# Gate steps four deep, one per piece, and lo products first in every other piece of a two-block network

## The chip, the cores and the metric

One core of one Trainium2 chip. The metric is device microseconds of one launch; lower is better. All weights come from HBM in float32 during the launch.

## What is computed

Two transformer-like blocks run on 256 tokens of width 2048. The part that the change touches is the expert layer of the second block: 16384 experts, of which each token uses 8 heads x 16. The kernel computes it densely.

```python
def peer(xn, w_pq, sub_k1, sub_k2, expert_u, expert_v):
    q = (xn @ w_pq).reshape(B, S, PEER_HEADS, 2, PEER_HALF)
    s1 = einsum('bshd,hnd->bshn', q[..., 0, :], sub_k1)
    s2 = einsum('bshd,hnd->bshn', q[..., 1, :], sub_k2)
    v1, i1 = top_k(s1, 16); v2, i2 = top_k(s2, 16)
    cand = v1[..., :, None] + v2[..., None, :]
    vs, ci = top_k(cand.reshape(..., 256), 16)
    eidx = e1 * 128 + e2            # e1, e2: entries of i1, i2 that ci names
    gates = softmax(vs)
    act = gelu(einsum('tkd,td->tk', expert_u[eidx], xb))
    return einsum('tk,tkd->td', act * gates, expert_v[eidx])
```

Before it stand a first block (three mixers, a feed-forward part of width 5632 with `w_up` and `w_dn`) and the attention of the second block; behind it a gated projection. None of that is changed, except that `w_up` uses the same product routine as the expert layer.

## The kernel before

**Products.** Every weight matrix is read in pieces of 512 KB (128 x 1024 float32). SyncE loads a piece into `raw` (line 327), ScalarE rounds it to `hi` (line 341), VectorE takes `lo = raw - hi` (line 342), and TensorE multiplies with the activations, which are split the same way. `get` (line 345) splits two pieces ahead; `raw`, `hi` and `lo` have three buffers each. In `mmH` (line 382; used by `w_up`, `w_pq` and `w_u`: 176, 32 and 256 pieces) a piece is 8 long products of 512 columns (line 390: `hi` times both halves of the activations) and then 8 short products of 256 columns (line 393: `lo` times the high half). Four pieces make one product [128, 2, 512] in `mm`; `sum_halves` (line 403) adds its halves with one ScalarE copy and two VectorE operations.

**Work beside the products.** `Background` holds generators (tasks). After each piece `pump` (line 71) lets them go on, in the order of the list, while two budgets last: `bg.rate` units (a rough cost in us) per piece for VectorE and as many for ScalarE. A plain `yield` hands back the turn within the same pump, `yield 1` waits for the next pump, and `finish` (line 98) runs a task to its end without a product in between. What the pump calls is written into the instruction queues at that point; each engine runs its queue in order.

**The expert layer** (`peer`, line 1832). Around the 32 pieces of `w_pq` and in the first part of `w_u` the routing runs: scores, top 16 (VectorE max, index and replace), pairs. Then `dense` makes the gates as a dense array of 256 tokens x 16384 experts in DRAM (`gdram`), in 64 steps of four tokens. One step: VectorE compares an iota with the tokens' indices (`AB`, 128 x 1024) and scales a quarter of it (128 x 256), ScalarE scales another quarter (two of 128 x 128), TensorE multiplies the two one-hot halves (line 1983: four float32 products of 128 columns, which the trace records as eight), ScalarE evicts `m` into `G`. Each fourth step completes a `G` of 1 MB, which ScalarE's queue stores to `gdram`. In the kernel before, the one-hot of step n+1 is made behind the product of step n, and the eviction of n behind that, with a plain `yield` between.

`peer_order` (line 1144): 16 quads of `w_u` (8 pieces each: 128 pieces), then the two products `v` with `w_v` (16 pieces each), then two quads and one `v` in turn. `gated` (line 2006) turns each quad's activations into factors of `v`: gelu on ScalarE, then, once all gates are stored, a load `Gq` from `gdram` by SyncE's queue, a VectorE product, and a split into `wh` and `wl`. At the first `v`, `finish` runs what is left of `dense`, then `gated` of quads 0 and 1.

Of the kernel before, what the change touches and what calls it, by code (L numbers as in the profile page):

```python
# [6 lines left out]
F32 = mybir.dt.float32  # L7
# [4 lines left out]
AF = mybir.ActivationFunctionType  # L12
# [235 lines left out]
class Net:  # L248
# [132 lines left out]

    def mmH(self, ps, hi, lo, k0, X, first, last):

        nc = self.nc
        kk, n = hi.shape[1:]
        kw = dict(skip_group_check=True)
        sl = [slice(c0, c0 + 128) for c0 in range(0, n, 128)]
        for i in range(kk):
            for c in range(n // 128):
                nc.tensor.matmul(ps[:, c], hi[:, i, sl[c]], X.both(k0 + i), start=first and i == 0, stop=False, **kw)  # L390
        for i in range(kk):
            for c in range(n // 128):
                nc.tensor.matmul(ps[:, c, 256:], lo[:, i, sl[c]], X(k0 + i)[0], start=False, stop=last and i == kk - 1, **kw)  # L393

    def prodH(self, name, X, nk, kk=4):
        ps = self.mm_ps([128, 2, 512])
# [1434 lines left out]
class Block3(Block2):  # L1831
    def peer(self, X):
        nc, V, S, G, A, bg, tc = self.nc, self.V, self.S, self.G, self.A, self.bg, self.tc
        V.fixed = 0.15
        bg.rate = 2.8
        h, st = self.h, self.st
        pa_ = ExitStack()
        pact = pa_.enter_context(tc.tile_pool(name="act", bufs=NACT))
# [92 lines left out]
        r_ = self.a4([128, 3, 256], name="routeT")  # L1931
# [23 lines left out]
        gst = {"ready": False}  # L1955

        def dense():

            yield lambda: t_route[3]
            rp_.close()  # L1960
            gp_ = gst["ctx"] = ExitStack()
            gp = gst["pool"] = gp_.enter_context(tc.tile_pool(name="gates", bufs=1, reuse_waits="tile"))
            def onehot(n):

                AB = gp.tile([128, 2, 4, 128], F32, name="AB", tag="AB", bufs=2)
                V.tensor_tensor(AB, self.iota[:, None, None, :].to_broadcast([128, 2, 4, 128]),
                                r_[:, 0:2, 4 * n:4 * n + 4, None].to_broadcast([128, 2, 4, 128]), op=OP.is_equal)
                V.tensor_mul(AB[:, 0, 0:2], AB[:, 0, 0:2], r_[:, 2, 4 * n:4 * n + 2, None].to_broadcast([128, 2, 128]))
                for i in (2, 3):
                    S.activation(AB[:, 0, i], AB[:, 0, i], AF.Copy, scale=r_[:, 2, 4 * n + i:4 * n + i + 1])  # L1970
                return AB

            bg.rate = 3.3
            nxt, full = onehot(0), None
            for n in range(64):
                if n % 4 == 0:
                    g = gp.tile([128, 128, 16], F32, name="G", tag="G", bufs=2)
                yield
                yield self.hold("m1")
                ps = self.m1([128, 4, 128])  # L1980
                AB = nxt
                for i in range(4):
                    nc.tensor.matmul(ps[:, i], AB[:, 1, i], AB[:, 0, i], start=True, stop=True)  # L1983
                if full is not None and n % 4 == 2:
                    nc.scalar.dma_start(self.gdram[n // 4 - 1], full.rearrange("p e t -> p (e t)"))
                    full = None
                if n < 63:
                    yield
                    nxt = onehot(n + 1)
                yield  # L1990
                S.activation(g[:, :, 4 * (n % 4):4 * (n % 4) + 4], ps.rearrange("p t e -> p e t"), AF.Copy)
                self.drop("m1")
                if n % 4 == 3:
                    full = g
            yield 1
            nc.scalar.dma_start(self.gdram[15], full.rearrange("p e t -> p (e t)"))
            yield 4
            gst["ready"] = True
            bg.rate = RATE

        t_route = bg.add(route())
        bg.add(dense())
        W, wt = {}, {}
        self.room.update(W=2, Gq=3)

        def gated(qd, a):
            S.activation(a, a, AF.Gelu_apprx_tanh)
            yield lambda: gst["ready"]
            yield self.hold("W")
            yield self.hold("Gq")  # L2010
            gq = gst["pool"].tile([128, 16, 4, 16], F32, name="Gq", tag="Gq", bufs=3)
            nc.sync.dma_start(gq.rearrange("p b e t -> p b (e t)"),
                              self.gdram.rearrange("b p n -> p b n")[:, :, 64 * qd:64 * qd + 64])
            yield 2
            V.tensor_mul(a.rearrange("p e (b t) -> p e b t", b=16), a.rearrange("p e (b t) -> p e b t", b=16),
                         gq.rearrange("p b e t -> p e b t"))
            self.drop("Gq")
            yield 1
            hi = self.a4([128, 4, 256], R32, "wh")
            lo = self.a4([128, 4, 256], R32, "wl")  # L2020
            S.activation(hi, a, AF.Copy)
            yield 1
            V.tensor_sub(lo, a, hi.bitcast(F32))
            W[qd] = hi, lo
# [4 lines left out]
        for kind, i in self.peer_order():  # L2029
            if kind == "u":  # L2030
                for z in range(2):
                    ps = self.prodH("w_u", X, 16)
                    if z == 0:
                        if i >= FIRST:
                            bg.finish(wt[i - NACT])
                        a = self.a4([128, 4, 256], name="act") if i < FIRST - NACT else pact.tile([128, 4, 256], F32, name="act")
                    self.sum_halves(a[:, 2 * z:2 * z + 2], ps, st["R4"])
                wt[i] = bg.add(gated(i, a))
                bg.tasks.insert(sum(not w[3] for w in wt.values()) - 1, bg.tasks.pop())
                continue  # L2040
            for qd in (2 * i, 2 * i + 1):
                bg.finish(wt[qd])
            Wf = lambda k: (W[2 * i + k // 4][0][:, k % 4], W[2 * i + k // 4][1][:, k % 4])
            for c in range(4):
                ps = self.prodB("w_v", Wf, 8)
                V.tensor_add(h[c], h[c], ps)
                if i == 15:
                    X5.make(c, lambda t, c=c: h[c][:, t], lambda j, c=c: self.col("g_ple", 4 * c + j),
                            before=self.squares(h[c], ssp[:, :, c:c + 1]))
            self.room["W"] += 4 if i == 1 else 2  # L2050
            del W[2 * i], W[2 * i + 1]
# [81 lines left out]
```

## Time and profile before

| | before |
|---|---|
| median of 3 runs | 3577.65 us (3572.88 to 3577.75) |
| the profiled execution's own time | 3569.16 us |
| its span, first to last instruction | 3567.4 us |
| mean granted TensorE clock | 0.994 of full speed |
| PE, DVE, ACT busy | 98%, 68%, 48% of the span |

A busy share is the mean over stages that have different limits. The layer in question runs from about 1850 us of the span to its end; the gate steps stand between 2137 and 2383 us. In a row of the timeline, "x8" is a group of eight instructions that follow each other; the number before the engine is the time from the first one's start to the last one's end, which overlaps the next group's start, so rates are read from start to start.

### The profile page before, as it was taken

The page shows a single profiled execution, that of the slowest core. Times are in us where ns is not written, and L with a number is a line of the kernel's source. Part 1 is how long each engine was busy: PE and PEld are TensorE (multiplying, and loading weights), DVE is VectorE, ACT ScalarE, POOL GpSimd, SP SyncE. Part 2 cuts the span into 40 slices and gives each one's busy share as a digit, 9 for nine tenths or more (in the row PEclk, how much of TensorE's full clock was granted, in tenths as well). Part 3 has the DMA queues.
Part 4 walks back from the last instruction along what each step waited for, and adds up shares of the span by engine and source line. Part 5 has one row for each costly group of instructions (what it writes and reads, how often), then busy time and mean ns, then how long its engine had stood idle before and what let it go on. Part 6 is the DMA issues. An engine that isn't in the chain of part 4 may idle for free.

```text
span 3567.4 us, 47459 instructions
## 1 busy us (share of the span) xinstructions
PE 3494.6 (98%) x18330; PEld 2983.6 (84%) x18330; DVE 2431.3 (68%) x3152; ACT 1712.7 (48%) x2100; POOL 268.9 (8%) x358
## 2 busy tenths in 40 slices
PE   8999999999999999999999999979999999999999
PEld 8788877888888888889788888867888888888887
DVE  7997675566775577667669987765656666666665
ACT  4345543445554455545554445543444444444453
POOL 6900000000000000020212000000000000000000
PEclk9999999999999999999999999989999999999999
DMA  6454554655566555665455555556766666667755
GB/s 227 152 162 161 171 171 141 198 199 184 188 201 194 190 191 186 193 192 176 135 171 180 186 183 178 189 175 195 214 206 202 201 202 203 205 203 216 220 189 183
DMA packets 244795, 670.05 MB, mean 188 GB/s; under 512 B 86181, under 2 KB 86629, under 8 KB 242393
## 3 DMA queue, kind: packets, MB, share of 16 engines
q1 hardware_dynamic: 239144, 639.59, 56.6%
q10 hardware_dynamic: 2736, 17.32, 1.2%
q0 software_dynamic: 2688, 10.12, 1.0%
q8 instruction: 143, 2.34, 0.3%
q14 instruction: 84, 0.68, 0.1%
HBM read 648.07 MB, written 18.87 MB: 187 GB/s over the span
## 4 chain that ended last, share of the span: by engine, by line
PE 90%; DVE 6%; ACT 1%; issue 1%; DMA 1%; SPq 0%; ACTq 0%; DVEq 0%
PE mm L362 32%; PE mm L390 22%; PE mm L366 16%; PE mm L393 11%; DVE lo L37 3%; PE mm L377 2%; PE m L1983 1%; DVE AB L37 1%; PE mm L380 1%; ACT hi L37 1%; PE m L494 1%; PE m L860 0%; PE m L377 0%; PE m L1018 0%; ACT AB L37 0%
## 5 line engine op out<-in xcount | busy, mean ns | idle before, releaser
L37 DVE TENSOR_TENSOR lo<-raw,hi 128x1024 fp32r<-128x1024 f32 (+1 forms) x1169 | 1430.9, 1230 | 789.8 <-ACT hi L37 771.5
L37 ACT ACTIVATE hi<-raw 128x1024 fp32r<-128x1024 f32 (+1 forms) x1185 | 1243.9, 1053 | 1285.0 <-PE mm L362 709.8
L390 PE MATMUL mm<-xt,hi 128*128 128x512 f32 x3712 | 936.0, 394 | 0.9 <-ACT hi L37 0.9
L390 PEld LDWEIGHTS mm<-xt,hi 128*128 128x128 f32 x3712 | 668.8, 189 | 121.6 <-ACT hi L37 1.3
L393 PEld LDWEIGHTS mm<-xt,lo 128*128 128x128 f32 x3712 | 506.3, 190 | 36.6
L393 PE MATMUL mm<-xt,lo 128*128 128x256 f32 x3712 | 517.3, 282 | 0.0
L362 PE MATMUL mm<-hi,wh 128*128 128x512 f32 x1024 | 401.0, 392 | 16.3 <-ACT wh L37 16.3
L362 PE MATMUL mm<-hi,wl 128*128 128x512 f32 x1024 | 400.6, 391 | 0.9 <-DVE wl L37 0.9
L362 PE MATMUL mm<-hi,x 128*128 128x512 f32 x1152 | 291.0, 395 | 2.8 <-ACT hi L37 2.8
L366 PE MATMUL mm<-lo,wh 128*128 128x512 f32 x1024 | 274.3, 390 | 0.0
L362 PEld LDWEIGHTS mm<-hi,x 128*128 128x128 f32 x1152 | 214.7, 189 | 49.6 <-ACT hi L37 3.2
L362 PEld LDWEIGHTS mm<-hi,wh 128*128 128x128 f32 x1024 | 193.4, 189 | 56.6 <-ACT wh L37 16.9
L362 PEld LDWEIGHTS mm<-hi,wl 128*128 128x128 f32 x1024 | 193.4, 189 | 41.8 <-DVE wl L37 1.9
L366 PEld LDWEIGHTS mm<-lo,wh 128*128 128x128 f32 x1024 | 193.0, 188 | 40.1
L362 PE MATMUL mm<-hi,xt 128*128 128x512 f32 x752 | 186.8, 390 | 0.1
L37 DVE TENSOR_TENSOR resid<-resid,mm 128x1024 f32<-128x1024 f32 x84 | 102.6, 1221 | 101.0 <-PE mm L366 101.0
L362 PEld LDWEIGHTS mm<-hi,xt 128*128 128x128 f32 x752 | 140.4, 188 | 29.3 <-issue 0.5
L366 PE MATMUL mm<-lo,x 128*128 128x512 f32 x576 | 155.0, 391 | 1.9 <-DVE lo L37 1.9
L362 PE MATMUL mm<-hi,acth 128*128 128x512 f32 x352 | 137.2, 390 | 0.0
L362 PE MATMUL mm<-hi,actl 128*128 128x512 f32 x352 | 137.0, 389 | 0.0
L366 PEld LDWEIGHTS mm<-lo,x 128*128 128x128 f32 x576 | 107.6, 188 | 26.6 <-DVE lo L37 4.2
L2066 POOL DMA_DIRECT2D pT<-in_pT_dram x1 | 0.6, 557 | 1447.9 <-PE mm L362 1447.9
(551 smaller groups left out, 3572.5 us busy)
## 6 DMA issues: line engine op xcount, KB each, us to landing
raw<-in_w_u_dram SPq DMA_DIRECT2D x256, 512.0 KB, 4.0
raw<-in_w_v_dram SPq DMA_DIRECT2D x256, 512.0 KB, 4.2
raw<-in_w_up_dram SPq DMA_DIRECT2D x176, 512.0 KB, 3.8
raw<-in_w_g_dram SPq DMA_DIRECT2D x96, 512.0 KB, 3.4
raw<-in_w_dn_dram SPq DMA_DIRECT2D x88, 512.0 KB, 4.2
raw<-in_w_o_dram SPq DMA_DIRECT2D x64, 512.0 KB, 3.5
raw<-in_w_b_dram SPq DMA_DIRECT2D x32, 512.0 KB, 3.5
raw<-in_w_br_dram SPq DMA_DIRECT2D x32, 512.0 KB, 3.9
```

The lines of the kernel that those rows point to most:

```text
L37: return f(*a, **k)
L362: nc.tensor.matmul(ps[:, t, :n], x[:, t * 128:t * 128 + 128], hi[:, i, :n], start=first and i == z == 0, stop=False)
L366: nc.tensor.matmul(ps[:, t, :n], X(k0 + i)[0][:, t * 128:t * 128 + 128], lo[:, i, :n], start=False, stop=last and i == kk - 1)
L377: nc.tensor.matmul(ps[:, c, :], hi[:, i, sl[c]], x, start=first and i == z == 0 and c % 2 == 0, stop=False, **kw)
L380: nc.tensor.matmul(ps[:, c, :], lo[:, i, sl[c]], X(k0 + i)[0], start=False, stop=last and i == kk - 1, **kw)
L390: nc.tensor.matmul(ps[:, c], hi[:, i, sl[c]], X.both(k0 + i), start=first and i == 0, stop=False, **kw)
L393: nc.tensor.matmul(ps[:, c, 256:], lo[:, i, sl[c]], X(k0 + i)[0], start=False, stop=last and i == kk - 1, **kw)
L494: self.nc.tensor.transpose(ps[:, c, t * 128:t * 128 + 128], src(t)[:, c * 128:c * 128 + 128], self.ident)
L1983: nc.tensor.matmul(ps[:, i], AB[:, 1, i], AB[:, 0, i], start=True, stop=True)
L2066: G.dma_start(p.rearrange("p a b -> p (a b)"), A["pT"])
```

## The change

Three parts:

- `dense` is written as a pipeline of single steps. At each step, with `yield 1` ahead of it: the product of step n, the compare and VectorE scale of step n+2, the eviction of step n-1, the ScalarE scale of step n+1. `AB` has three buffers, `Gq` two (before: two and three).
- `bg.rate` during the routing is 3.0 (before: 2.8).
- `mmH`: in each odd piece of a product the short `lo` products come first, then the long ones; even pieces stay as they were.

```diff
--- before.py
+++ after.py
@@ -381,16 +381,18 @@
 
     def mmH(self, ps, hi, lo, k0, X, first, last):
 
+
         nc = self.nc
         kk, n = hi.shape[1:]
         kw = dict(skip_group_check=True)
         sl = [slice(c0, c0 + 128) for c0 in range(0, n, 128)]
-        for i in range(kk):
-            for c in range(n // 128):
-                nc.tensor.matmul(ps[:, c], hi[:, i, sl[c]], X.both(k0 + i), start=first and i == 0, stop=False, **kw)
-        for i in range(kk):
-            for c in range(n // 128):
-                nc.tensor.matmul(ps[:, c, 256:], lo[:, i, sl[c]], X(k0 + i)[0], start=False, stop=last and i == kk - 1, **kw)
+        for long in (False, True) if k0 // kk % 2 else (True, False):
+            for i in range(kk):
+                for c in range(n // 128):
+                    if long:
+                        nc.tensor.matmul(ps[:, c], hi[:, i, sl[c]], X.both(k0 + i), start=first and i == 0, stop=last and i == kk - 1, **kw)
+                    else:
+                        nc.tensor.matmul(ps[:, c, 256:], lo[:, i, sl[c]], X(k0 + i)[0], start=False, stop=False, **kw)
 
     def prodH(self, name, X, nk, kk=4):
         ps = self.mm_ps([128, 2, 512])
@@ -1832,7 +1834,7 @@
     def peer(self, X):
         nc, V, S, G, A, bg, tc = self.nc, self.V, self.S, self.G, self.A, self.bg, self.tc
         V.fixed = 0.15
-        bg.rate = 2.8
+        bg.rate = 3.0
         h, st = self.h, self.st
         pa_ = ExitStack()
         pact = pa_.enter_context(tc.tile_pool(name="act", bufs=NACT))
@@ -1962,38 +1964,53 @@
             gp = gst["pool"] = gp_.enter_context(tc.tile_pool(name="gates", bufs=1, reuse_waits="tile"))
             def onehot(n):
 
-                AB = gp.tile([128, 2, 4, 128], F32, name="AB", tag="AB", bufs=2)
+                AB = ab[n] = gp.tile([128, 2, 4, 128], F32, name="AB", tag="AB", bufs=3)
                 V.tensor_tensor(AB, self.iota[:, None, None, :].to_broadcast([128, 2, 4, 128]),
                                 r_[:, 0:2, 4 * n:4 * n + 4, None].to_broadcast([128, 2, 4, 128]), op=OP.is_equal)
                 V.tensor_mul(AB[:, 0, 0:2], AB[:, 0, 0:2], r_[:, 2, 4 * n:4 * n + 2, None].to_broadcast([128, 2, 128]))
+
+            def scale(n):
                 for i in (2, 3):
-                    S.activation(AB[:, 0, i], AB[:, 0, i], AF.Copy, scale=r_[:, 2, 4 * n + i:4 * n + i + 1])
-                return AB
-
-            bg.rate = 3.3
-            nxt, full = onehot(0), None
-            for n in range(64):
+                    S.activation(ab[n][:, 0, i], ab[n][:, 0, i], AF.Copy, scale=r_[:, 2, 4 * n + i:4 * n + i + 1])
+
+            def evict(n):
+                nonlocal g, full
                 if n % 4 == 0:
                     g = gp.tile([128, 128, 16], F32, name="G", tag="G", bufs=2)
-                yield
-                yield self.hold("m1")
-                ps = self.m1([128, 4, 128])
-                AB = nxt
-                for i in range(4):
-                    nc.tensor.matmul(ps[:, i], AB[:, 1, i], AB[:, 0, i], start=True, stop=True)
-                if full is not None and n % 4 == 2:
-                    nc.scalar.dma_start(self.gdram[n // 4 - 1], full.rearrange("p e t -> p (e t)"))
-                    full = None
-                if n < 63:
-                    yield
-                    nxt = onehot(n + 1)
-                yield
-                S.activation(g[:, :, 4 * (n % 4):4 * (n % 4) + 4], ps.rearrange("p t e -> p e t"), AF.Copy)
+                S.activation(g[:, :, 4 * (n % 4):4 * (n % 4) + 4], ps.pop(n).rearrange("p t e -> p e t"), AF.Copy)
                 self.drop("m1")
                 if n % 4 == 3:
                     full = g
-            yield 1
-            nc.scalar.dma_start(self.gdram[15], full.rearrange("p e t -> p (e t)"))
+
+            def store(b):
+                nc.scalar.dma_start(self.gdram[b], full.rearrange("p e t -> p (e t)"))
+
+
+            bg.rate = 3.3
+            ab, ps, g, full = {}, {}, None, None
+            onehot(0)
+            yield 1
+            onehot(1)
+            scale(0)
+            for n in range(64):
+                yield 1
+                yield self.hold("m1")
+                ps[n] = self.m1([128, 4, 128])
+                AB = ab.pop(n)
+                for i in range(4):
+                    nc.tensor.matmul(ps[n][:, i], AB[:, 1, i], AB[:, 0, i], start=True, stop=True)
+                if n % 4 == 2 and n > 4:
+                    store(n // 4 - 1)
+                if n + 2 < 64:
+                    onehot(n + 2)
+                if n:
+                    evict(n - 1)
+                if n + 1 < 64:
+                    scale(n + 1)
+            yield 1
+            evict(63)
+            yield 1
+            store(15)
             yield 4
             gst["ready"] = True
             bg.rate = RATE
@@ -2001,14 +2018,14 @@
         t_route = bg.add(route())
         bg.add(dense())
         W, wt = {}, {}
-        self.room.update(W=2, Gq=3)
+        self.room.update(W=2, Gq=2)
 
         def gated(qd, a):
             S.activation(a, a, AF.Gelu_apprx_tanh)
             yield lambda: gst["ready"]
             yield self.hold("W")
             yield self.hold("Gq")
-            gq = gst["pool"].tile([128, 16, 4, 16], F32, name="Gq", tag="Gq", bufs=3)
+            gq = gst["pool"].tile([128, 16, 4, 16], F32, name="Gq", tag="Gq", bufs=2)
             nc.sync.dma_start(gq.rearrange("p b e t -> p b (e t)"),
                               self.gdram.rearrange("b p n -> p b n")[:, :, 64 * qd:64 * qd + 64])
             yield 2
```

What this does to the queues is seen at three places. TensorE's queue at the end of the first 128 pieces of `w_u` (`mm` with `xt`: products of a piece; `m1` with `AB`: gate steps; `wh`, `wl`: the first `v`), before:

```order
L390 MATMUL mm_20279<-xt_15528,hi_20304 128x512 x4
L390 MATMUL mm_20279<-xt_15529,hi_20304 128x512 x4
L393 MATMUL mm_20279<-xt_15528,lo_20305 128x256 x4
L393 MATMUL mm_20279<-xt_15529,lo_20305 128x256 x4
L1983 MATMUL m1_20403<-AB_20375 128x128 x4
L1983 MATMUL m1_20419<-AB_20409 128x128 x4
L1983 MATMUL m1_20431<-AB_20424 128x128 x4
L1983 MATMUL m1_20442<-AB_20436 128x128 x4
L1983 MATMUL m1_20453<-AB_20447 128x128 x4
L1983 MATMUL m1_20465<-AB_20459 128x128 x4
L362 MATMUL mm_20486<-hi_20349,wh_20475 128x512
```

and changed:

```order
L2001 MATMUL m1_20407<-AB_20340 128x128 x4
L393 MATMUL mm_20350<-xt_15407,hi_20353 128x512 x4
L393 MATMUL mm_20350<-xt_15408,hi_20353 128x512 x4
L395 MATMUL mm_20350<-xt_15407,lo_20354 128x256 x4
L395 MATMUL mm_20350<-xt_15408,lo_20354 128x256 x4
L2001 MATMUL m1_20438<-AB_20378 128x128 x4
L395 MATMUL mm_20350<-xt_15528,lo_20388 128x256 x4
L395 MATMUL mm_20350<-xt_15529,lo_20388 128x256 x4
L393 MATMUL mm_20350<-xt_15528,hi_20387 128x512 x4
L393 MATMUL mm_20350<-xt_15529,hi_20387 128x512 x4
L362 MATMUL mm_20486<-hi_20418,wh_20475 128x512
```

Before, six of the 64 steps stand together behind the last piece, and elsewhere none to two behind one piece; changed, one step stands behind each of the 64th to the 127th of the 128 pieces, and none behind the last. The first step stands behind the 74th of the 128 pieces before, and behind the 64th now. In the odd pieces (here the last one) `lo` comes first.

ScalarE's queue at the same end (`G`: evictions; `AB`: ScalarE's scaling; `act`: `sum_halves` and gelu of the last quad; `gdram`: a store; `wh`: the first factor of `v`), before:

```order
L37 ACTIVATE AB_20424<-AB_20424,routeT_16463 128x128 x2
L37 ACTIVATE G_20336<-m1_20419 128x128x4
L37 ACTIVATE AB_20436<-AB_20436,routeT_16463 128x128 x2
L37 ACTIVATE G_20430<-m1_20431 128x128x4
L37 ACTIVATE AB_20447<-AB_20447,routeT_16463 128x128 x2
L37 ACTIVATE G_20430<-m1_20442 128x128x4
L1985 DMA gdram_59<-G_20336 128x2048
L37 ACTIVATE AB_20459<-AB_20459,routeT_16463 128x128 x2
L37 ACTIVATE G_20430<-m1_20453 128x128x4
L37 ACTIVATE G_20430<-m1_20465 128x128x4
L1996 DMA gdram_59<-G_20430 128x2048
L37 ACTIVATE wh_20475<-act_16580 128x1024
```

and changed:

```order
L37 ACTIVATE hi_20387<-raw_20385 128x1024
L1986 DMA gdram_59<-G_20242 128x2048
L37 ACTIVATE G_20381<-m1_20373 128x128x4
L37 ACTIVATE AB_20378<-AB_20378,routeT_16477 128x128 x2
L37 ACTIVATE hi_20418<-raw_20416 128x1024
L37 ACTIVATE G_20381<-m1_20407 128x128x4
L37 ACTIVATE hi_20446<-raw_20444 128x1024
L37 ACTIVATE G_20381<-m1_20438 128x128x4
L37 ACTIVATE act_20346<-mm_20350 128x512
L37 ACTIVATE act_20346<-act_20346 128x1024
L1986 DMA gdram_59<-G_20381 128x2048
L37 ACTIVATE wh_20475<-act_16604 128x1024
```

Before, the last store stands right behind the last eviction (the copy and the gelu of the last quad come earlier, above the rows shown); now that copy and gelu stand between the last eviction and the last store (line 1986).

SyncE's queue a little later, at the first quads of `w_u` behind the two products `v`, before:

```order
L327 DMA raw_21093<-in_w_u_dram 128x1024
L2012 DMA Gq_21115<-gdram_59 128x16x64
L2012 DMA Gq_21117<-gdram_59 128x16x64
L2012 DMA Gq_21119<-gdram_59 128x16x64
L327 DMA raw_21121<-in_w_u_dram 128x1024
```

and changed:

```order
L327 DMA raw_21093<-in_w_u_dram 128x1024
L2029 DMA Gq_21115<-gdram_59 128x16x64
L2029 DMA Gq_21117<-gdram_59 128x16x64
L327 DMA raw_21119<-in_w_u_dram 128x1024
L327 DMA raw_21141<-in_w_u_dram 128x1024
```

Two loads of gates follow each other instead of three, and the third has gone to a later place.

## Rows read from the trace of the kernel before

**Rows 1.** The page, part 1: busy us, share of the span, instructions.
```profile
PE 3494.6 (98%) x18330; PEld 2983.6 (84%) x18330; DVE 2431.3 (68%) x3152; ACT 1712.7 (48%) x2100; POOL 268.9 (8%) x358
```
**Rows 2.** Stretches: length, busy us (xinstructions) by engine, PEclk, DMA share, GB/s.
```profile
2000.00:2100.00 100.00, 100.00 (x575) 88.02 (x574) 92.96 (x182) 47.08 (x50) 0.00 (x0) 1.00 0.59 189
2137.00:2396.00 259.00, 220.78 (x1388) 197.36 (x1386) 185.78 (x213) 142.87 (x269) 0.00 (x0) 0.96 0.52 179
```
**Rows 3.** Waits from 2135.4 to 2396 us: total us, times, longest.
```profile
PE m L1983 <- ACT AB L37: 19.2, 21, 3.0
...
PE mm L362 <- ACT wh L37: 12.8, 1, 12.8
```
**Rows 4.** Timeline of PE without gate steps: start, us, instructions.
```profile
2056.61 2.00 PE L390 MATMUL mm<-xt,hi 128*128 128x512 f32 x8
```
**Rows 5.** Timeline of PE: start of the gate stage, and two pieces with unhindered steps.
```profile
2135.49 2.00 PE L390 MATMUL mm<-xt,hi 128*128 128x512 f32 x8
...
2146.59 2.09 PE L390 MATMUL mm<-xt,hi 128*128 128x512 f32 x8
...
2150.28 2.09 PE L390 MATMUL mm<-xt,hi 128*128 128x512 f32 x8
```
**Rows 6.** Timeline, one piece with a hindered step ([idle before <-releaser]).
```profile
2161.90 2.09 PE L390 MATMUL mm<-xt,hi 128*128 128x512 f32 x8
...
2164.63 0.69 ACT L37 ACTIVATE AB<-AB,routeT 128x128 f32<-128x128 f32 x2 [2.00 <-DVE AB L37]
2165.14 1.13 PE L1983 MATMUL m<-AB 128*128 128x128 f32 x8 [0.20 <-ACT AB L37]
...
2166.03 2.10 PE L390 MATMUL mm<-xt,hi 128*128 128x512 f32 x8
```
**Rows 7.** Timeline at the end of the gate stage, ACT, queues, DVE, PE.
```profile
2372.65 0.57 ACT L37 ACTIVATE act<-mm 128x512 f32<-128x512 f32 x1
...
2374.71 1.06 ACT L37 ACTIVATE act<-act 128x1024 f32<-128x1024 f32 x1 [1.48 <-DVE act L37]
...
2383.09 0.60 ACT L37 ACTIVATE G<-m 128x512 f32<-128x512 f32 x1 [0.56 <-PE m L1983]
2383.72 0.33 ACTq L1996 DMA_DIRECT2D gdram<-G  x1
2388.62 1.63 SPq L2012 DMA_DIRECT2D Gq<-gdram  x2
...
2393.45 1.23 DVE L37 TENSOR_TENSOR act<-act,Gq 128x1024 f32<-128x1024 f32 x1 [11.67 <-DMA Gq<-gdram]
2394.71 1.06 ACT L37 ACTIVATE wh<-act 128x1024 fp32r<-128x1024 f32 x1 [11.02 <-DVE act L37]
...
2395.82 0.79 PE L362 MATMUL mm<-hi,wh 128*128 128x512 f32 x1 [12.76 <-ACT wh L37]
```
**Rows 8.** Timeline of PE, stretches of 256 columns alone and of 512 columns alone.
```profile
102.20 2.08 PE L377 MATMUL mm<-x,hi 128*128 128x256 f32 x16
...
105.08 2.08 PE L377 MATMUL mm<-x,hi 128*128 128x256 f32 x16
...
302.49 1.98 PE L362 MATMUL mm<-hi,x 128*128 128x512 f32 x8
...
305.21 1.98 PE L362 MATMUL mm<-hi,x 128*128 128x512 f32 x8
```
**Rows 9.** Timeline in the routing stage: end of a product, a split, the next pieces.
```profile
2098.51 2.00 PE L390 MATMUL mm<-xt,hi 128*128 128x512 f32 x8
...
2098.72 0.60 ACT L37 ACTIVATE act<-mm 128x512 f32<-128x512 f32 x1 [2.69 <-PE mm L393]
...
2099.35 1.21 DVE L37 TENSOR_TENSOR lo<-raw,hi 128x1024 fp32r<-128x1024 f32 x1
...
2101.31 2.00 PE L390 MATMUL mm<-xt,hi 128*128 128x512 f32 x8
```
**Rows 10.** Timeline of SyncE's queue behind the first two products v.
```profile
2486.18 6.18 SPq L2012 DMA_DIRECT2D Gq<-gdram  x3
```

## Prediction

> **What bounds the kernel now.** I read the page's busy times first, then stretches, waits and the timeline. TensorE is busy for 3494.6 of 3567.4 us [rows 1], so time can only come out of its 73 idle us, out of its half-clock stretches, or out of the spacing of its matmuls; of the other engines only their lateness counts. The routing stage gives nothing: from 2000 to 2100 us TensorE is busy all the time, while VectorE is busy for 92.96 of 100 us [rows 2]. The gate stage does give something: from 2137 to 2396 us TensorE is busy for 220.78 of 259 us, at a mean clock of 0.96 [rows 2]. Two kinds of wait stand there: matmuls of a gate step for ScalarE's scaling of `AB` (19.2 us in 21 waits), and one of 12.8 us at the end for `wh` [rows 3].
>
> **What the gate stage loses.** A piece without a step takes (2101.31 - 2056.61) / 16 = 2.794 us [rows 4, 9]. A piece with an unhindered step takes 2150.28 - 2146.59 = 3.69 us [rows 5], so a step costs TensorE 0.90 us. The stage runs from the start of the 74th piece of `w_u`, ahead of the first step, to the first matmul of `v`: 2395.82 - 2135.49 = 260.3 us [rows 5, 7]. In it lie 55 pieces and 64 steps: 55 x 2.794 + 64 x 0.90 = 211.3 us of work. The loss is 49.0 us: 12.8 at the end, 36 inside (waits of steps, the six steps behind the last piece, and some half-clock stretches).
>
> **Part 1, the pipeline of steps.** Where a step is hindered, compare, scale and product of one step follow each other within one piece: the period is 2166.03 - 2161.90 = 4.13 us, since ScalarE's scaling begins at 2164.63 and the matmuls start at 2165.14 [rows 6]. Changed, a step's compare, scale, product and eviction stand in four successive pieces, so each has about one period of slack. What an engine must do in a period of 3.69 us fits, by the durations of rows where there are any and by the number of elements else: VectorE has a split and a compare of 1024 elements at 1.23 each (as the product of that size [rows 7]), a scale of a quarter (0.4), and per product two operations (0.7 each, a quarter of them per piece): 3.2 us. ScalarE has a split of 1.06, an eviction of 0.60, scales of 0.69, and a share of copies and gelus (0.3) [rows 6, 7]: 2.7 us. TensorE remains the bound, and 36 us go to almost nothing. I take 1 us of remaining waits inside; the bounds are 0 and 64 x (4.13 - 3.69) = 28 us, if every step stays hindered, and I choose the low end because the rows without a wait [rows 5] need less slack than the new order gives.
>
> At the end the wait does not go, it grows. What is late next is the chain from the last gates to the first `wh`: from the store's issue at 2383.72 by way of store (4.9), load (4.8), product and split to the matmul at 2395.82 it is 12.10 us [rows 7]. Before, the store follows the last eviction, and that the last step. Now the last step is hidden behind the last piece, but in ScalarE's queue the copy and the gelu of the last quad stand ahead of the store. The copy can start only 0.21 us after the last piece (2098.72 against 2098.51 [rows 9]); from its start to the gelu's end it takes 2374.71 + 1.06 - 2372.65 = 3.12 us [rows 7], since VectorE adds and multiplies between. So TensorE idles 0.21 + 3.12 + 12.10 = **15.4 us** there. The half-clock stretch behind it stays and is not counted on either side.
>
> Part 1: 15.4 + 1 - 49.0 = **-32.6 us**.
>
> **Part 2, the order of products.** 24 matmuls of 256 columns (16 and the 8 behind them) take 105.08 - 102.20 = 2.88 us, so 0.120 each; 12 of 512 columns (8 and 4) take 305.21 - 302.49 = 2.72 us, so 0.227 each [rows 8]. A piece has eight of each: 8 x 0.347 = 2.774 us, but it takes 2.794. The 0.020 us I put down to the change from short to long products and back. With `lo` first in odd pieces long meets long and short meets short, and half of these changes go. Of 464 pieces 400 have no gate step between them and the next: 200 x 0.020 = **-4.0 us**. Bounds: 0, if the 20 ns are the price of something else (the strided halves of the activations, say), and -8, if both pieces of a pair gain. I take -4, since 8 + 8 of one kind is the only difference from the rows of one kind.
>
> The Trainium skill speaks against this part (TensorE: Matmul & The Clock Gate, section "Back-to-back issue gap"): the isolated gap of a warm matmul is given there as columns / 2.4 plus 2.5 ns, by which order is free and this term would be 0. The rows differ from that formula already within one kind (227 and 120 ns, where it gives 216 and 109).
>
> The new order has a price too: an odd piece needs its `lo` when it begins, 8 x 0.23 = 1.84 us earlier than before. In the routing stage that is close: the split that begins at 2099.35 ends at 2100.56, and its piece, an odd one, begins at 2101.31, 0.75 us later [rows 9]. Still in time, so no cost by itself.
>
> **Part 3, 3.0 instead of 2.8.** It lets the first step come behind the 64th piece instead of the 74th; without it the steps would not all fit ahead of the last piece. VectorE's load rises to 0.93 x 3.0 / 2.8 = 0.996 of TensorE's time [rows 2]: covered on the mean, with no reserve, and the lead of 0.75 us is thin. Bounds: 0, and 0.2 us for each of some 58 pieces, 11.6 us, if all that is added is late. I take **+2 us**, near the low end, since the load stays below 1 and splits are two pieces ahead.
>
> **Buffers.** The third `AB` is what the pipeline needs; two `Gq` suffice for one `v` (two quads). Three loads held SyncE's queue for 6.18 us [rows 10], two hold raw pieces back less; the next pair comes later. I count 0, within 1 us either way.
>
> **Sum.** -32.6 - 4.0 + 2 = -34.6 us against the profiled execution's 3569.16, so 3534.6. The median of the runs shown, 3577.65, lies 8.5 above that execution, so on its scale I forecast **3543 us**, 1% faster.
>
> **Rivals.**
> - *The order of products is free* (chance 0.14). By the mechanism above the 20 ns would belong to the long products themselves. For it: they also read two halves at once. Then -30.6, 3547 us. The skill's formula, named above, is on this side.
> - *VectorE runs out in the routing* (0.12). All that is added is late: 11.6 instead of 2, so -25.0, 3553 us. For it: 0.996; against it: no wait of TensorE in the stage before [rows 2].
> - *The steps stay hindered* (0.07): the pipeline does not do what it says, 28 us remain instead of 1: -7.5, 3570 us. For it only that each step still has four engine changes; against it the slack worked out above.
> - *Slower: `lo` first makes every odd piece wait for VectorE* (0.04). Place: the 45 odd pieces of `w_pq` and `w_u` in the routing stage, where VectorE is full. If its lag lasts, each waits up to the 1.84 us by which its `lo` is wanted earlier: 83 us less the 34.6, 3577.65 + 48 = 3626 us. It decides from 34.6 / 45 = 0.77 us per odd piece. Against it: that the lead at such pieces is positive, 0.75 us, and the load stays below 1.
>
> The forecast itself has 0.63. Its own range is 3537 to 3549.
>
> **How the numbers follow.** The low end is no loss in the routing, none inside the stage, and up to 6 us for the order of products: about -40, and some us for the spread of the medians (the three runs differ by 5 us): 3534. The high end takes in the first two rivals and a few us inside the stage besides: 3560. Outside lie the last two rivals and a little of the forecast, some 0.15. About 0.2%, 7 us, is what a measurement of this kernel can tell from no change. Faster by more than that: the forecast, the first two rivals and half of the third, 0.92; within it: 0.04, the other half; slower: 0.04.
>
> **What would show it.** In the profile after: the waits of `m` for `AB` fall from 19.2 us to about 1; the wait of the first `v` matmul for `wh` grows from 12.8 to about 15.4 us; the pieces with steps stand 3.69 us apart from first to last; two successive pieces without a step take 5.57 instead of 5.59 us; VectorE is busy for over 97 of 100 us in the routing, with a few us of waits of TensorE for `lo`. I am wrong in part 1 if a wait of steps for ScalarE or VectorE remains at each product's end, in part 2 if pairs of pieces keep their 5.59 us, and in part 3 if TensorE waits for `lo` by more than 5 us in the routing.

## The result, and the profile after

| | before | after |
|---|---|---|
| median of four runs | 3576.47 us (3572.88 to 3577.75) | 3535.99 us (3532.41 to 3538.03) |
| the profiled execution's own time | 3569.16 us | 3535.07 us |
| its span | 3567.4 us | 3533.2 us |
| mean granted clock | 0.994 | 0.995 |

The ratio is 0.9892 (95% interval 0.9879 to 0.9905): 40 us faster by the medians, 34.1 by the profiled executions, for which the forecast had 34.6. The two differences need not agree. The profiled execution of before lies 7 us below its median, that of after only 1 us below. And the profiled execution of after lost some time ahead of everything that was changed: its first matmul of `w_up` starts at 830.70 us, that of before at 827.42, 3.3 us earlier. From there to the end after is 37.5 us shorter.

Stretches of after (us; then busy time and instructions of PE, PE's weight loads, VectorE, ScalarE, GpSimd; granted clock, DMA share, GB/s): the routing, the pieces with gate steps.

```profile
2000.00:2100.00 100.00, 97.97 (x559) 85.71 (x558) 93.10 (x179) 49.65 (x53) 0.00 (x0) 1.00 0.56 180
...
2114.00:2350.00 236.00, 236.00 (x1539) 214.84 (x1539) 194.66 (x221) 154.19 (x277) 0.00 (x0) 1.00 0.61 207
```

All TensorE waits of after from 1850 to 2400 us (us in total, times, longest):

```profile
PE mm L362 <- ACT wh L37: 13.2, 1, 13.2
PE mm L395 <- DVE lo L37: 2.2, 3, 1.3
PE mm L362 <- DVE wl L37: 0.5, 1, 0.5
```

Before had one more line in the stretch of [rows 3]:

```profile
PE m L1983 <- DVE AB L37: 6.3, 4, 2.7
```

So the 19.2 us of gate products that waited for ScalarE [rows 3] are gone, and so are these 6.3 us in which they waited for VectorE's `AB`. In the stretch with gate steps TensorE is busy for 236.00 of 236 us at full clock; before, for 220.54 of 246 at 0.98 (the line is shown in the part on why the prediction was right; the 259 us of [rows 2] take in the wait at the end as well). The wait for the first `wh` stayed, and a small new wait for `lo` stands in the routing.

The timeline of after at the end of the stage (start, length, engine, idle before and its releaser) answers to [rows 7]:

```profile
2347.38 1.20 PE L395 MATMUL mm<-xt,lo 128*128 128x256 f32 x8
2347.66 0.60 ACT L37 ACTIVATE G<-m 128x512 f32<-128x512 f32 x1 [0.74 <-PE m L2001]
2348.42 2.00 PE L393 MATMUL mm<-xt,hi 128*128 128x512 f32 x8
2350.46 0.60 ACT L37 ACTIVATE act<-mm 128x512 f32<-128x512 f32 x1 [2.19 <-PE mm L393]
2352.54 1.06 ACT L37 ACTIVATE act<-act 128x1024 f32<-128x1024 f32 x1 [1.48 <-DVE act L37]
2352.54 0.33 ACTq L1986 DMA_DIRECT2D gdram<-G  x1
2356.46 1.80 SPq L2029 DMA_DIRECT2D Gq<-gdram  x2
2361.25 1.22 DVE L37 TENSOR_TENSOR act<-act,Gq 128x1024 f32<-128x1024 f32 x1 [8.75 <-DMA Gq<-gdram]
2362.51 1.06 ACT L37 ACTIVATE wh<-act 128x1024 fp32r<-128x1024 f32 x1 [8.91 <-DVE act L37]
2363.61 0.80 PE L362 MATMUL mm<-hi,wh 128*128 128x512 f32 x1 [13.20 <-ACT wh L37]
```

The last gates leave `m` at 2347.66 to 2348.26, under the last piece. But their store starts at 2352.54, behind the copy of the last quad in ScalarE's queue. From there 11.07 us pass to the first matmul of `v`: store 3.92, load 4.79, product, split.

### The profile page after: what moved, and what is told of

Same layout as the page of the kernel before. It is cut to its first block, busy times and chain, and to the rows that moved or that the text cites. A ratio compares the mean times of both kernels' runs of the same rounds, so it can differ in the third digit from the quotient of the medians.

```text
span 3533.2 us, 47465 instructions
## 1 busy us (share of the span) xinstructions
PE 3480.0 (98%) x18330; PEld 2977.2 (84%) x18330; DVE 2433.0 (69%) x3152; ACT 1716.4 (49%) x2102; POOL 270.1 (8%) x358
## 4 chain that ended last, share of the span: by engine, by line
PE 92%; DVE 5%; DMA 1%; issue 1%; ACT 1%; SPq 0%; DVEq 0%; ACTq 0%
PE mm L362 31%; PE mm L393 23%; PE mm L366 16%; PE mm L395 12%; DVE lo L37 2%; PE mm L377 2%; PE m L2001 2%; PE mm L380 1%; PE m L496 1%; PE m L862 0%; ACT hi L37 0%; DVE s L37 0%; PE m L377 0%; PE m L1020 0%; DMA raw<-in_w_a_dram 0%
## 5 line engine op out<-in xcount | busy, mean ns | idle before, releaser
L393 PE MATMUL mm<-xt,hi 128*128 128x512 f32 x3712 | 898.4, 392 | 0.0
L393 PEld LDWEIGHTS mm<-xt,hi 128*128 128x128 f32 x3712 | 679.2, 188 | 129.3
L395 PEld LDWEIGHTS mm<-xt,lo 128*128 128x128 f32 x3712 | 478.2, 191 | 21.3 <-DVE lo L37 3.1
L395 PE MATMUL mm<-xt,lo 128*128 128x256 f32 x3712 | 491.2, 283 | 2.2 <-DVE lo L37 2.2
```

## The experiments

The median of before in their sessions was 3571.89 to 3572.9 us. Medians of four or five runs that lie less than some 4 us apart I don't call different. In the table, "waits" is the sum of all TensorE waits from 1850 to 2400 us of the profiled execution; it is free of what happens elsewhere in the kernel.

| kernel | median, us | ratio to before | waits, us |
|---|---|---|---|
| before | 3571.89 to 3576.47 | 1 | 38.8 |
| after | 3535.99 | 0.9892 [0.9879, 0.9905] | 15.9 |
| after, run again | 3535.45 | 0.9898 [0.9883, 0.9913] | 16.1 |
| before + order alone | 3568.41 | 0.9992 [0.9983, 1.0002] | 38.3 |
| before + pipeline and buffers, rate 2.8 | 3541.01 | 0.9914 [0.9901, 0.9928] | 16.1 |
| before + rate 3.0 alone | 3559.46 | 0.9965 [0.9951, 0.9978] | 28.6 |
| after, old order | 3539.52 | 0.9912 [0.9897, 0.9927] | 16.6 |
| after, rate 2.8 | 3535.51 | 0.9902 [0.9887, 0.9917] | 16.9 |
| after, rate 3.1 | 3528.30 | 0.9884 [0.9869, 0.99] | 9.0 |
| after, rate 3.2 | 3532.04 | 0.9887 [0.987, 0.9903] | 11.5 |
| after, two `AB` | 3535.85 | 0.9897 [0.9881, 0.9914] | 15.6 |
| after, store early | 3530.68 | 0.9885 [0.9868, 0.9901] | 12.1 |
| after, 3.1 and store early | 3528.77 | 0.988 [0.9865, 0.9895] | 9.2 |
| after, half of `lo` on GpSimd | 3537.19 | 0.9898 [0.9882, 0.9915] | 17.0 |

### The order of products alone

Only the change's part of `mmH`, in the kernel before:

```diff
-        for i in range(kk):
-            for c in range(n // 128):
-                nc.tensor.matmul(ps[:, c], hi[:, i, sl[c]], X.both(k0 + i), start=first and i == 0, stop=False, **kw)
...
+        for long in (False, True) if k0 // kk % 2 else (True, False):
+            for i in range(kk):
+                for c in range(n // 128):
+                    if long:
...
```

> The kernel before with the new order of products alone (part 2). My theory: a change from short to long products costs about 20 ns, 200 of them go: 4 us less than before, and pairs of pieces without a step 5.57 us apart instead of 5.59. Rival, the order is free: 0, and 5.59. Second rival, lo first makes odd pieces wait for VectorE: slower by up to 0.8 us per odd piece of the routing, with waits of TensorE for lo in the trace; at 2.8 units I expect none of them, but one or two behind the first two products v, where three loads of gates hold the queue.

By the medians (3.5 us less) it isn't told from no change. The traces tell it, since only the spacing of rows is needed. Timeline of TensorE in `w_up`, before, where the pieces carry no gate step:

```profile
1216.55 2.00 PE L390 MATMUL mm<-xt,hi 128*128 128x512 f32 x8
...
1222.14 2.00 PE L390 MATMUL mm<-xt,hi 128*128 128x512 f32 x8
```

The same of before with the new order:

```profile
1217.06 3.82 PE L393 MATMUL mm<-xt,hi 128*128 128x512 f32 x16
...
1222.63 3.82 PE L393 MATMUL mm<-xt,hi 128*128 128x512 f32 x16
...
1233.76 3.82 PE L393 MATMUL mm<-xt,hi 128*128 128x512 f32 x16
```

Two pieces took 1222.14 - 1216.55 = 5.59 us; three pairs now take 1233.76 - 1217.06 = 16.70, or 5.567 each. Some 0.02 us per pair, for 200 pairs, is 4 us, the term as forecast. The whole of the trace agrees: the first matmul of `w_up` starts at 827.42 us before and at 830.68 with the new order, but the span is 3567.4 and 3566.3 us, so from `w_up` to the end the order gains 4.4 us. No wait for `lo` came into the routing; one of 0.9 us stands behind the first two products `v`, as expected. The Trainium skill (TensorE: Matmul & The Clock Gate, section "Back-to-back issue gap") gives a gap for an isolated warm matmul that depends on its columns alone; by that the two spacings would be equal, and this trace, with 5.59 and 5.567, differs.

### The change without the order

After, with `mmH` as it was before:

```diff
-        for long in (False, True) if k0 // kk % 2 else (True, False):
-            for i in range(kk):
-                for c in range(n // 128):
-                    if long:
...
+        for i in range(kk):
+            for c in range(n // 128):
+                nc.tensor.matmul(ps[:, c], hi[:, i, sl[c]], X.both(k0 + i), start=first and i == 0, stop=False, **kw)
...
```

> The changed kernel with the old order of products. My theory: it gives back the 4 us of part 2, but some of the waits of TensorE for lo in the routing (2.2 us in the changed kernel) go with the early lo: 1 to 4 us slower than the changed kernel, 34 to 37 us faster than before. Rival, the order is free: equal to the changed kernel or up to 2 us faster than it.

It ran at 3539.52, 4.1 us above after run again: the same size from the other side, though hardly more than these medians tell apart. Against before it gains 32.4 us, where I had expected 34 to 37. Its waits of TensorE from 1850 to 2400 us:

```profile
PE mm L362 <- ACT wh L37: 13.4, 1, 13.4
PE m L1950 <- DVE e L37: 1.4, 1, 1.4
PE mm L393 <- DVE lo L37: 1.3, 1, 1.3
```

So 2.7 us of waits for VectorE stand in the routing without `lo` first, as against 2.2 with it. They belong to the rate, not to the order.

### The pipeline alone, and the rate alone

The pipeline alone is after, with `mmH` as before (the edit of the run above) and this:

```diff
-        bg.rate = 3.0
+        bg.rate = 2.8
```

> Part 1 alone: the kernel before with the pipeline of steps and its buffers, old order, 2.8 units. My theory after the run with 2.8 units: the pipeline carries nearly the whole gain; against before it wins 49 - 12.3 (end) - 5.3 (ten uncovered steps) - 1 = 30 us, so 3540 to 3543 where before is 3572. Rival: it needs the 3.0 units, and wins less than 20 us alone.

The rate alone is before, with this:

```diff
-        bg.rate = 2.8
+        bg.rate = 3.0
```

> Part 3 alone: the kernel before with 3.0 units. The first step stands behind the 63rd piece, the last behind the 122nd. My theory: the end wait is covered by six pieces (12.8 us go, and 2 us of a slow start), the six uncovered steps go (5 to 8 us), hindered steps inside stay (25 to 30 us) and 2 us of waits for lo come: 15 to 20 us faster than before. Rival, the waits only move into the stage: within 5 us of before.

The pipeline alone brings 31.0 of the 36.6 us that after brought in the same session; the rate alone 12.6. The rate alone still leaves most hindered steps; waits of before with 3.0, from 2095 to 2400 us:

```profile
PE m L1983 <- ACT AB L37: 17.8, 17, 3.0
PE mm L362 <- ACT wh L37: 6.4, 1, 6.4
PE m L1983 <- DVE AB L37: 1.6, 1, 1.6
```

12.6 is less than the 15 to 20 that I expected: the wait for `wh` falls by 6.4 us, not by all of its 12.8, though the last step now stands behind the 122nd piece. 4.7 us go in waits for VectorE's `AB`, the waits for scaling fall only from 19.2 to 17.8, and 2.3 us of waits come into the routing. The pipeline with 2.8 loses all 21 waits for ScalarE's scaling and keeps the one at the end:

```profile
PE mm L362 <- ACT wh L37: 11.8, 1, 11.8
PE m L1999 <- ACT G L37: 1.9, 1, 1.9
PE m L1999 <- DVE AB L37: 1.9, 4, 0.5
```

31.0 and 12.6 are not added up: both pay for the same loss of the gate stage.

### The change with 2.8

```diff
-        bg.rate = 3.0
+        bg.rate = 2.8
```

> The changed kernel with 2.8 units during the routing (part 3 undone). The first step then stands behind the 75th piece and about ten steps behind the last. My theory: the ten steps run uncovered, each as long as VectorE's compare and scale (1.65 us), so 13 to 17 us slower than the changed kernel, less 2 to 3 us of waits in the routing that go: 3546 to 3550. Rival, the rate does not matter because the pipeline alone does it: within 3 us of the changed kernel.

My expectation fell; the rival was right: 3535.51, by the medians the same as after. The first step now stands behind the 75th piece, so ten steps lack a piece to hide behind. Timeline of this kernel behind the last piece:

```profile
2332.91 1.95 PE L2001 MATMUL m<-AB 128*128 128x128 f32 x16
...
2346.47 1.13 PE L2001 MATMUL m<-AB 128*128 128x128 f32 x8 [0.47 <-DVE AB L37]
2348.06 1.13 PE L2001 MATMUL m<-AB 128*128 128x128 f32 x8 [0.46 <-DVE AB L37]
...
2349.86 0.33 ACTq L1986 DMA_DIRECT2D gdram<-G  x1
```

The last uncovered steps follow each other at 2348.06 - 2346.47 = 1.59 us, of which 0.90 is TensorE's work, due in any place: such a step costs 0.7, not 1.6. The ten together take 2348.06 - 2332.91 = 15.15 us, 6.2 more than their own work, and 1.9 of that is one wait for an eviction. Against this, the copy and the gelu of the last quad now run beside these steps, so the wait for `wh` is 12.2 instead of 13.2, and the 2.2 us of waits in the routing are absent. The waits add up to 16.9 us, as against 15.9. From the same matmul ahead of the layer to the first of `v` this kernel takes 2361.36 - 1851.17 = 510.19 us and after 2363.61 - 1855.12 = 508.49: 3.0 units win 1.7 us there, less than medians tell apart.

### Further up: 3.1 and 3.2

```diff
-        bg.rate = 3.0
+        bg.rate = 3.1
```

and the same with 3.2.

> The changed kernel with 3.1 units: the last step stands four pieces earlier. My theory: about 11 us of the wait at the end (13.2 in the changed kernel) go behind pieces; VectorE is asked for more than TensorE's time in the routing (0.93 x 3.1 / 2.8 = 1.03), which costs 0.03 x 2.79 x some 90 pieces = 7 us more waits for lo, less what two pieces of lead absorb: 3 to 9 us faster than the changed kernel. Rival, VectorE is full and every unit of rate costs its whole price: as fast as the changed kernel or slower by up to 5 us.

> The changed kernel with 3.2 units: the last step stands eight pieces earlier than in the changed kernel. My theory: the wait at the end goes altogether (13.2 and 2 to 3 us behind it), VectorE is asked for 1.06 of TensorE's time in the routing: 10 to 15 us of waits there, less the lead; between 5 us faster than the changed kernel and equal. Rival, VectorE has slack that the busy share does not show: 13 us faster or more.

With 3.1 the last step stands behind the 123rd piece; the run is 7 us faster than after, and the waits are 6.9 us less. Waits from 1850 to 2400 us, with 3.1:

```profile
PE mm L362 <- ACT wh L37: 4.4, 1, 4.4
PE mm L395 <- DVE lo L37: 1.9, 3, 1.3
PE m L1952 <- DVE e L37: 1.9, 1, 1.9
```

and with 3.2:

```profile
PE mm L362 <- DVE wl L37: 3.7, 1, 3.7
PE mm L395 <- DVE lo L37: 3.6, 4, 1.4
PE m L1875 <- DVE qT L37: 2.9, 2, 1.4
PE m L1952 <- DVE e L37: 1.3, 1, 1.3
```

With 3.2 the last step stands behind the 119th piece, four pieces earlier, and it gains little: the wait at the end is 3.7 instead of 4.4 (now for `wl`), while the routing pays 7.8 us of waits for VectorE instead of 3.8 (I had expected 10 to 15). The gates are early enough with 3.1; what still waits at the end is told below.

### Two `AB` instead of three

```diff
-                AB = ab[n] = gp.tile([128, 2, 4, 128], F32, name="AB", tag="AB", bufs=3)
+                AB = ab[n] = gp.tile([128, 2, 4, 128], F32, name="AB", tag="AB", bufs=2)
```

> The changed kernel with two AB buffers instead of three. My theory: the compare of step n+2 then waits for the product of step n, at the end of its piece, and still has a period of slack ahead of its own product: at most 3 us slower than the changed kernel. Rival, the third buffer carries the gain: VectorE is held up at each product's end (4.3 us of work against a period of 3.69), 0.5 us or more for each of 16 products, 8 us or more slower.

No cost: 3535.85, and TensorE still never waits in the stage:

```profile
2114.00:2350.00 236.00, 236.00 (x1540) 214.84 (x1539) 195.64 (x221) 156.53 (x277) 0.00 (x0) 1.00 0.60 207
```

The compare of step n+2 waits with two buffers until the product of step n is done, but that product is issued ahead of it in the same piece.

### The last store ahead of the last quad

The task `dense` is finished ahead of `sum_halves` of the last quad:

```diff
-        bg.add(dense())
+        t_dense = bg.add(dense())
...
+                    if i == FIRST - 1 and z == 1:
+                        bg.finish(t_dense)
```

> The changed kernel with the last store put into ScalarE's queue ahead of the copy and the gelu of the last quad. My theory: the store starts about 4 us earlier (right behind the last eviction, near 2348.3 instead of 2352.5 us), so the wait for wh falls from 13.2 to about 9 us: 4 us faster than the changed kernel. Rival, the wait is not set by the store but by the queue that loads the gates: no difference.

Timeline of this kernel:

```profile
2348.65 0.33 ACTq L1986 DMA_DIRECT2D gdram<-G  x1
...
2350.81 0.60 ACT L37 ACTIVATE act<-mm 128x512 f32<-128x512 f32 x1 [2.19 <-PE mm L393]
...
2359.44 0.79 PE L362 MATMUL mm<-hi,wh 128*128 128x512 f32 x1 [8.67 <-ACT wh L37]
```

The store starts right behind the last eviction and 2.16 us ahead of the copy. The end wait falls from 13.20 to 8.67, the median by 5 us. This shows that the queue's order, not the gates, set the last part of that wait.

### Both: 3.1 and the early store

```diff
-        bg.rate = 3.0
+        bg.rate = 3.1
```

together with the edit of the run above.

> The changed kernel with 3.1 units and with the last store ahead of the copy and gelu (the edits of the two best runs together). My theory: they act on the same wait at the end (4.4 us are left of it with 3.1 units), so they do not add up: the earlier store is four pieces away from the last copy by then and wins at most 1 us over 3.1 units alone. Rival, they add up: the wait is gone and with it the slow start, 6 to 8 us faster than 3.1 units alone.

3528.77, as 3.1 alone: not additive. Its timeline at the end, with the wait for `wh` still 4.36 us:

```profile
2346.26 3.36 SPq L2029 DMA_DIRECT2D Gq<-gdram  x2
...
2354.74 0.69 DVE L37 TENSOR_TENSOR act<-act,R 128x512 f32<-128x512 f32 x1
2355.35 1.22 DVE L37 TENSOR_TENSOR act<-act,Gq 128x1024 f32<-128x1024 f32 x1
```

The load is issued at 2346.26, and the gated product of the first quad follows at once behind the last operation of `sum_halves` of the last quad. It waits for VectorE's queue, and so for the last piece, not for gates. This is the floor that the order of these queues sets.

### Half of `lo` on GpSimd

In the first quads of `w_u`, `split` gives half of its `lo` to GpSimd:

```diff
-        self.share = False
...
+            self.share = kind == "u" and i < 8
```

> The changed kernel with half of the lo splits on GpSimd during the first 8 quads of w_u too (as in w_pq). The first step stands behind the 50th piece then, the last behind the 113th. My theory: the wait at the end goes (13.2 us, and 2 to 3 us of a slow start behind it) and so do the waits for lo in the routing (2.2 us): 16 to 18 us faster than the changed kernel. Rival: GpSimd and VectorE hinder each other (in w_pq six products of 128x512 on VectorE took 1.79 us in the mean instead of 0.69), lo comes late, and TensorE waits in the routing for 10 us or more: no gain, or slower.

The rival was right: 3537.19, no gain. All steps are in time and the wait for `wh` is gone, but TensorE waits for `lo`:

```profile
PE mm L395 <- DVE lo L37: 15.6, 5, 7.5
```

Groups of VectorE and GpSimd in the routing, 1975 to 2100 us (count, busy us, mean ns, idle before), of this kernel:

```profile
L342 POOL TENSOR_TENSOR lo<-raw,hi 128x1024 fp32r<-128x1024 f32 x19 | 49.3, 2597 | 79.0 <-ACT hi L37 79.0
...
L37 DVE TENSOR_TENSOR lo<-raw,hi 128x1024 fp32r<-128x1024 f32 x18 | 25.9, 1441 | 2.4 <-ACT hi L37 2.4
...
L37 DVE TENSOR_TENSOR cand<-io,abf 128x512 f32<-128x512 f32 x12 | 16.5, 1377 | 0.3
```

and of after:

```profile
L37 DVE TENSOR_TENSOR lo<-raw,hi 128x1024 fp32r<-128x1024 f32 x44 | 52.8, 1218 | 5.2 <-ACT hi L37 5.1
...
L37 DVE TENSOR_TENSOR cand<-io,abf 128x512 f32<-128x512 f32 x12 | 8.3, 689 | 0.2
```

GpSimd does a split in 2597 ns on the mean. VectorE's sums `cand` take 1377 ns instead of 689 and its own splits 1441 instead of 1218, but these means mix two cases. Eight of the twelve sums still took 0.69 us; the other four took 2.56 to 2.90, and each of them had a split of GpSimd beside it and ended 0.55 us behind that split's end. One of the four in the timeline of this kernel:

```profile
2045.41 1.22 DVE L37 TENSOR_TENSOR lo<-raw,hi 128x1024 fp32r<-128x1024 f32 x1
2045.61 3.27 POOL L342 TENSOR_TENSOR lo<-raw,hi 128x1024 fp32r<-128x1024 f32 x1 [1.39 <-ACT hi L37]
2046.54 2.89 DVE L37 TENSOR_TENSOR cand<-io,abf 128x512 f32<-128x512 f32 x1
```

The Trainium skill (SBUF — State Buffer, section "SBUF: two separate sides") calls the pair of ports that the two engines share an exclusive lock: of a VectorE operation with two SBUF inputs and a GpSimd operation that reads SBUF, the one that starts second is blocked until the first is done. The trace agrees in both directions: VectorE's split, which began first, kept its 1.22 us, and GpSimd's, which began 0.20 us later, took 3.27 instead of some 2.4; the sum behind it ended only after GpSimd's split did.

### The change run again

After, with no edit.

> The changed kernel itself once more, beside the others, to have its time on the same chip and day: 3531 to 3536 where before is 3572.

3535.45 against 3535.99: the medians that the runs above are held against.

## Why the prediction was right, step by step

- **Inside the stage.** Forecast 36 us of loss down to 1. Measured 0: TensorE busy for 236.00 of 236.00 us. Of before's loss 25.5 us were the waits for `AB`: 19.2 for ScalarE, and 6.3 for VectorE, a third kind of wait where the prediction named two. The other 10 or so are no wait: they lie in TensorE's busy time. About half of them is the granted clock: before, it was 0.83 from 2250 to 2260 us, 0.72 from 2320 to 2326 and 0.66 from 2375 to 2380, together some 10 us at 1.2 of 2.4 GHz, which cost 5 us at most; now it is 1.00 throughout. The rest fits the hindered steps themselves: the piece of [rows 6] is 0.44 us longer than an unhindered one, but only 0.20 is recorded as a wait; 25 times the other 0.24 is 6 us, an estimate. The stretch of before, its gate steps alone:

```profile
2137.00:2383.00 246.00, 220.54 (x1387) 197.17 (x1385) 184.36 (x211) 141.22 (x267) 0.00 (x0) 0.98 0.51 177
```

- **The end wait.** Forecast: it grows from 12.8 to 15.4. Measured 13.2 by the wait, and 13.4 as the forecast counts it (first `v` matmul at 2363.61; the last piece's eight long matmuls begin at 2348.42 and, at 0.23 each, end near 2350.25). The copy starts 0.2 us after that end, as forecast. The term was 2 us too big in two places: I put the store behind the *end* of the gelu, and it starts with the gelu's start (2352.54 both, 1.06 us), and the store took 3.92 instead of 4.9.
- **The order.** Forecast -4.0. The spacing gives 4, the order alone 4.4 from `w_up` on (0.6 of it a shorter wait for `wh`), two pairs of medians 4 and 5.5 (3539.52 to 3535.45, 3541.01 to 3535.51). I had left out the pieces with steps, which gain too. Between these two rows of after lie 63 of them:

```profile
2115.55 2.07 PE L393 MATMUL mm<-xt,hi 128*128 128x512 f32 x8
...
2347.38 1.20 PE L395 MATMUL mm<-xt,lo 128*128 128x256 f32 x8
```

That is (2347.38 - 2115.55) / 63 = 3.680 us each; with the old order the first and the last step start at 2118.80 and 2351.48, 3.693 each. Over 64 pieces it makes another 0.8 us.
- **The rate.** The waits for `lo` are 2.2 us, where I had +2. But my reason for it fell: I wrote that without 3.0 the steps would not all fit ahead of the last piece. They don't, and it costs little: the ten uncovered steps cost 6.2 us beyond their own work, most of it is paid by a shorter end wait and no waits in the routing, and 1.7 us are left in the traces, nothing by the medians. VectorE's average in the routing did not rise to over 97 either: 93.10 of 100 in the stretch of [rows 2]. The price shows in three single waits, not in the mean.
- **Buffers.** Wrong in words, without weight: the third `AB` carries nothing. The two `Gq` cost nothing and win up to 0.9 us: from 2440 to 2560 us TensorE waits for a split in the three traces with three `Gq` (before: 0.9 for `hi`; order alone: 0.9 for `lo`; rate alone: 0.2 for `hi`), and in after and the two runs of it with the old order it doesn't.
- **Rivals.** "The order is free" is refuted by the spacings; "VectorE runs out" by 2.2 us of waits instead of 11.6; "steps stay hindered" by 236.00 of 236; "`lo` first waits in the routing" by the change with the old order, whose waits there are as long.
- **The sum.** Against the profiled executions 34.6 to 34.1. The mechanism holds, but that the sum came so close is luck, for errors of opposite sign met: the stage lost 49.0 and now 13.4 (-35.6), the order gave 4 and 0.8, the waits for splits 0.9, the routing took 2.2, together -39.1; 3.3 us came back ahead of `w_up`, in work that the change doesn't touch; 1.7 us are not assigned. The median, 3535.99, lies 7 us below the 3543 forecast, since I carried over the 8.5 us between before's profiled execution and its median, and after has only 0.9. So it lies within the range of 3534 to 3560, but 1 us below the forecast's own 3537 to 3549.

## What to carry to other kernels

In this kernel a step whose stages run on different engines costs the bound engine only its own work once each stage stands one period ahead of its use; read that from the rows of an unhindered step, not from averages. A step that loses its cover costs only what exceeds the bound engine's own work (here 0.7 of 1.6 us; ten such steps 6.2 us), and what would have followed it can hide beside it. When the steps are covered, look at the queue order of the last chain: the early store alone brought 5 us and 3.1 units alone 7, but both together no more than 7, since the next item in VectorE's queue took over.

## What the runs showed of the hardware

A DMA in ScalarE's queue did not wait for the end of the activation ahead of it: the store of `G` and the gelu both begin at 2352.54, and the gelu takes 1.06 us. Of the 16 stores of `G` 15 begin during an activation in before, and all 16 in after. I had taken the two in sequence.

Eight long after eight short products cost some 0.02 us per pair of pieces more than sixteen and sixteen (5.59 and 5.567). And beside GpSimd's splits VectorE's sum of two 128 x 512 inputs was not slowed by a share: it took its usual 0.69 us, or, when it began during such a split, as long as the split still ran and 0.55 us more (2.56 to 2.90). From 1975 to 2100 us both engines together made 37 splits, VectorE alone 44.
